# A new stripe order at the end of an input projection, and a denser weave of modulation columns

## The chip, the cores and the metric

The kernel runs on one core of one Trainium2 chip. The metric is the device time of one execution in microseconds; lower is better.

## The reference, cut to what matters

One encoder layer is applied with the same weights to a prompt (512 tokens) and a sample (1024 tokens), both 1024 wide. Everything is float32; the kernel holds activations transposed, channels on the partitions.

```
mod = silu(c) @ w_ada + b_ada        # 6 x 1024 per request: shift, scale, gate for mixer and MLP
h   = rmsnorm(x) * (1 + scale_a) + shift_a
[q | k | v | u] = h @ w_in           # 1280 columns = 10 stripes of 128
q, k = rope(rmsnorm per head)        # 8 query heads, 2 key heads, 64 wide
a   = softmax(q k^T / 8) v           # bidirectional
p   = (centred window mean of u - u) @ w_pool * pool_scale
x   = x + gate_a * rmsnorm([a | p] @ w_out)
x   = x + gate_m * rmsnorm(relu(h2 @ w_ff1)^2 @ w_ff2)
```

## The kernel before, in words

Big products are split: weights and activations are each a high and a low part (`wh`, `wl`; `hh`, `hl`), and `block` (L154) adds three 128x512 matmuls for each 128 rows of the contraction: L159 (wh, high), L160 (wh, low), L161 (wl, high). A 128x512 output of 1024 inner rows is 24 matmuls.

The stage that the change touches lies between 102 and 300 us. Three generators are woven together there by `weave`, which advances a background by its rate each time the foreground yields (after every six matmuls):

- the foreground `in_proj_s` (L567), the sample's input projection: 10 stripes of `w_in` in the order of `S_IN`, two halves of 512 tokens each, 20 blocks of 24 matmuls. Stripes 0 to 3 are queries, 4 the keys, 5 the values, 6 to 9 the pooling channels u. A query stripe is followed by `qk_post` (L386): ScalarE copies the block out of PSUM (L377, `xT`), TensorE transposes it (L383, `nat`, in `ps_m` or, every second time, in one half of `s2`), ScalarE squares (L393), VectorE norms and rotates in seven larger operations (L395 to L410, `y`), TensorE transposes back (L383), ScalarE and VectorE split it (L414, L415, `rh`), and ScalarE's queue writes it to DRAM (L419, `q_d`). A pooling stripe is only copied out and written to DRAM (L584, `u_d`).
- `bg`, at a rate of 1.2: `attention(0)`, the prompt's attention, 16 units of two heads. A head's half of a unit is: scores S (L618, two matmuls into the one tile `s2`), a maximum on VectorE (L628, `amx`), an exponential on ScalarE (L630, `p`), the reciprocal (L632) and the scaling by it on ScalarE or VectorE (L634, L636), four transposes on TensorE (L653, `pT`), a split (L656 `ph` on ScalarE, L657 `pl` on VectorE). A unit then ends with eight matmuls with the values (L666, L667, `x`), a copy (L671, `ao`) and a write to DRAM (L672, `a_d`). All of `s2` is one tile: the next scores, and every transpose that `qk_post` puts in its other half, wait for the exponential that reads it.
- `gv`, at a rate of 0.38: `gemv_cols`, 24 columns of the prompt's modulation (the first five steps are empty). A column is one 512 KB load (L268, `g`) and one 128x1024 multiply-and-sum on VectorE (L236).

Behind the weave stand `drain(bg)`, `drain(gv)`, and the prompt's output projection: `out_prep` (L720) reads `p_d` and `a_d` back (L741, L733), adds two halves on VectorE (L734) and splits (`oh` L743, `ol` L744); `out_proj(0, 0)` (L749) is eight blocks of 24 matmuls on these, with `attention(1)`, the sample's attention, woven in at 0.5. Its first scores need the load `q` (L602) of the sample's queries, into a buffer that the prompt's attention had.

The order on each engine is not the order of the code: a scheduler lays the instructions out when the program is built, each engine then runs its own list in order, and an instruction that waits holds up what stands behind it, on a queue that issues DMAs as well. SP issues the loads, ScalarE's queue the writes.

Of the kernel before, what the change touches and what calls it, by code (L numbers as in the profile page):

```python
# [24 lines left out]
def weave(fg, bgs):  # L25

    credit = [0.0] * len(bgs)
    for _ in fg:
        for i, (bg, rate) in enumerate(bgs):
            credit[i] += rate  # L30
            while credit[i] >= 1.0:
                credit[i] -= 1.0
                next(bg, None)


def drain(g):
    for _ in g:
        pass


def chain(*gs):
    for g in gs:
        yield from g
# [3 lines left out]
def hymba_encoder_layer(ctx, tc, xp, xs, ns_, vec, gqk, rope, edge, ident_in, w_ada_c,  # L47
# [99 lines left out]
    def next_w():  # L147

        while w_seq and len(w_ready) < AHEAD + 1:
            w_ready.append(load_w(*w_seq.pop(0)))  # L150
        return w_ready.pop(0)

    def mm_tile():
        return ps_mm.tile([128, 512], F32, tag="mm", name="mm")  # L154

    def block(ps, wh, wl, acts, ks=range(KB)):
        for i, k in enumerate(ks):
            ah, al = acts[k]
            nc.tensor.matmul(ps, lhsT=wh[:, k, :], rhs=ah, start=(i == 0), stop=False)  # L159
            nc.tensor.matmul(ps, lhsT=wh[:, k, :], rhs=al, start=False, stop=False)  # L160
            nc.tensor.matmul(ps, lhsT=wl[:, k, :], rhs=ah, start=False, stop=(i == len(ks) - 1))  # L161
            if i % 2 or i == len(ks) - 1:
                yield
# [94 lines left out]
    def gemv_cols(c, cb, lo=16, hi=48, pool=None):  # L258
        late = []
        for jb in range(lo, hi):  # L260
            if pool is None:
                r = load_raw(w_ada_c[jb])
                gemv_part(c, jb, r, cb, r)
                if jb % 8 == 7:
                    gemv_done(c, jb - 7)
            else:
                r = pool.tile([128, 1024], F32, tag="g", name="g", bufs=2)
                dma(r, w_ada_c[jb])  # L268
                tc.keep_in_program_order(gemv_part(c, jb, r, cb, r))
                if late:  # L270
                    gemv_done(c, late.pop())
                if jb % 8 == 7:
                    late.append(jb - 7)
            yield
        for j0 in late:
            gemv_done(c, j0)
# [98 lines left out]
    def evac(ps, t=None):  # L375
        t = inp.tile([128, 528], F32, tag="pl", name="xT", bufs=3)[:, :512] if t is None else t
        nc.scalar.activation(out=t, in_=ps, func=AF.Copy)  # L377
        return t
# [47 lines left out]
    def v_post(c, hf, xT):  # L426
        t = natural(xT)
        tv = t.rearrange("p (j h d) -> p j h d", j=4, h=2)
        vh = vst[c][:, hf * 4:hf * 4 + 4, :, 0, :]
        vl = vst[c][:, hf * 4:hf * 4 + 4, :, 1, :]  # L430
        nc.scalar.activation(out=vh, in_=tv, func=AF.Copy)
        nc.vector.tensor_tensor(vl, tv, vh.bitcast(F32), AL.subtract)
        yield
# [128 lines left out]
            posts.append(qk_post(0, 0, xs_[b], b))  # L562
        rest.append(rp)

    S_IN = (4, 5, 9, 0, 8, 1, 7, 2, 6, 3)

    def in_proj_s():  # L567
        pend = []
        ws = {}
        for blk, hf in [(b, f) for f in range(2) for b in S_IN[:3]] + [(b, f) for b in S_IN[3:] for f in range(2)]:  # L570
            if hf == 0:
                ws[blk] = next_w()
            wh, wl = ws[blk]
            ps = mm_tile()
            for _ in block(ps, wh, wl, [h_t[1, hf, k] for k in range(KB)]):
                if pend and next(pend[0], 1) == 1:
                    pend.pop(0)
                yield
            if blk < 5:
                pend.append(qk_post(1, hf, evac(ps), blk))  # L580
            elif blk == 5:
                pend.append(v_post(1, hf, evac(ps)))
            else:
                put(u_d[blk - 6, :, hf * 512:(hf + 1) * 512], evac(ps))  # L584
        while pend:
            if next(pend[0], 1) == 1:
                pend.pop(0)
            yield
# [693 lines left out]
    hs0, hs1 = hs[8:14] + hs[0:2], hs[2:8] + hs[14:16]  # L1282
    w_seq += [(w_in[b],) for b in S_IN]
    w_seq += [(w_out[m],) for m in range(KB)]
# [13 lines left out]
    bg = attention(0, att0)  # L1298
    gv = gemv_cols(0, cb0, 16, 40, inp)
    gv = chain([0] * 5, gv)  # L1300
    bg = chain([0] * 6, bg)
    weave(in_proj_s(), [(bg, 1.2), (gv, 0.38)])
    drain(bg)
    drain(gv)
    att0_close()
# [17 lines left out]
    bg = attention(1, att1)  # L1323
# [10 lines left out]
    def gemv_rest():  # L1334
        make_cb(0, cb[:, 0:1024])
        yield from gemv_cols(0, cb[:, 0:1024], 40)
        make_cb(1, cb[:, 0:1024])
        yield from gemv_cols(1, cb[:, 0:1024])
        for g in range(4):
            yield from u_post(1, g, (cb[:, 0:528], cb[:, 528:1056]))  # L1340
    gv = gemv_rest()
# [160 lines left out]
```

## Time and profile before

| what | us |
|---|---|
| median of 3 runs (lowest, highest) | 1666.7 (1665.64, 1670.02) |
| the profiled execution's own time | 1668.83 |
| its span, from first to last instruction | 1665.7 |
| TensorE busy / VectorE / ScalarE in the span | 1611.2 / 1213.7 / 854.8 |

In the profile a line names an engine, a source line, an operation, and what it writes and reads by the program's names; buffer numbers are left out there (`s2` reads `s`, `hh0_3` reads `hh`). "Idle before" is the time the engine stood still ahead of the instruction, and behind the arrow stands what ended it. PEld is the weight load of TensorE, which runs beside its matmuls. SPq and ACTq are the issuing of DMAs on those two queues. PEclk is the clock that TensorE was granted, 1.00 being full speed. Times within the span count from its start.

### The profile page before, as it was taken

The numbers are of one execution on the slowest core, as the hardware profiler recorded it, in microseconds if no ns is written. First come the engines' busy times: TensorE is split into PE (matmuls) and PEld (weight loads), VectorE is DVE, ScalarE is ACT, GpSimd is POOL, SyncE is SP. The second block draws the span as 40 slices with busy tenths as digits, with TensorE's granted clock in tenths as the row PEclk, the third lists the DMA queues.
The fourth block names the chain that finished last, engine by engine and source line by source line (L and its number), as shares of the span: only waits on it lengthen the run. The fifth ranks groups of instructions, "written<-read, shape, count | busy, mean of one in ns | idle before, by whom it ended". The sixth has DMA issues, their size and how long they took to land. (4 is left out here: it accounts for less than half of the span.)

```text
span 1665.7 us, 21550 instructions
## 1 busy us (share of the span) xinstructions
PE 1611.2 (97%) x7680; PEld 1299.9 (78%) x7680; DVE 1213.7 (73%) x1938; ACT 854.8 (51%) x1450; POOL 10.4 (1%) x27
## 2 busy tenths in 40 slices
PE   7999998999999999999999999899999999999996
PEld 4467886788888878888888888788888788888886
DVE  7898988568667675655667487878875576878757
ACT  2446664556645545546453475744445564444433
POOL 0000000000000000000000000000000000000002
PEclk8999999989999999999999999999999999999998
DMA  7756776443555553332368537566663745444334
GB/s 294 279 156 186 224 221 183 146 153 123 166 174 180 165 179 102 100 108 89 99 206 245 178 127 246 195 224 226 225 216 121 237 160 186 140 141 152 93 110 152
DMA packets 150618, 287.57 MB, mean 173 GB/s; under 512 B 15152, under 2 KB 56432, under 8 KB 150512
## 3 DMA queue, kind: packets, MB, share of 16 engines
q1 hardware_dynamic: 125824, 258.31, 47.9%
q10 hardware_dynamic: 24688, 27.89, 5.4%
q8 instruction: 60, 0.98, 0.2%
q14 instruction: 46, 0.38, 0.1%
HBM read 223.20 MB, written 61.37 MB: 171 GB/s over the span
## 5 line engine op out<-in xcount | busy, mean ns | idle before, releaser
L140 DVE TENSOR_TENSOR wl<-raw,wh 128x1024 fp32r<-128x1024 f32 (+2 forms) x106 | 121.1, 1142 | 70.4 <-ACT wh L139 69.9
L139 ACT ACTIVATE wh<-raw 128x1024 fp32r<-128x1024 f32 (+2 forms) x106 | 105.4, 995 | 120.4 <-PE mm L160 91.7
L630 ACT ACTIVATE p<-s,amx 128x1024 f32<-128x1024 f32 (+1 forms) x96 | 93.3, 972 | 108.6 <-DVE amx L628 106.7
L657 DVE TENSOR_TENSOR pl<-pT,ph 128x512 fp32r<-128x512 f32 x160 | 108.6, 686 | 54.8 <-ACT ph L656 54.3
L875 PE MATMUL pa<-fo,wh 128*128 128x512 f32 x448 | 140.4, 395 | 2.7 <-ACT x L1012 2.7
L628 DVE TENSOR_REDUCE amx<-s 128x1 f32<-128x1024 f32 (+1 forms) x96 | 100.1, 1042 | 43.5 <-PE s L618 43.1
L656 ACT ACTIVATE ph<-pT 128x512 fp32r<-128x512 f32 x160 | 93.4, 594 | 46.1 <-PE pT L653 36.8
L159 PE MATMUL mm<-hA,wh 128*128 128x512 f32 x256 | 106.7, 417 | 0.0
L159 PE MATMUL mm<-fh,wh 128*128 128x512 f32 x256 | 106.5, 417 | 0.0
L875 PE MATMUL mm<-fo,wh 128*128 128x512 f32 x336 | 104.8, 393 | 0.0
L875 PEld LDWEIGHTS pa<-fo,wh 128*128 128x128 f32 x448 | 84.8, 189 | 21.9 <-ACT x L1012 3.1
L161 PE MATMUL mm<-fh,wl 128*128 128x512 f32 x256 | 101.3, 396 | 0.0
L160 PE MATMUL mm<-fl,wh 128*128 128x512 f32 x256 | 101.0, 394 | 0.0
L160 PE MATMUL mm<-hA,wh 128*128 128x512 f32 x256 | 100.9, 395 | 0.0
L161 PE MATMUL mm<-hA,wl 128*128 128x512 f32 x256 | 100.5, 394 | 0.0
L653 PE MATMUL pT<-ident,p 128*128 128x128 f32 x640 | 96.6, 275 | 1.4 <-DVE pl L657 0.9
L618 PE MATMUL s<-kst,q 128*128 128x512 f32 x320 | 93.9, 406 | 4.0 <-ACT p L630 2.0
L653 PEld LDWEIGHTS pT<-ident,p 128*128 128x128 f32 x640 | 79.3, 142 | 22.6 <-issue 2.4
L875 PE MATMUL pa<-fo,wl 128*128 128x512 f32 x224 | 88.1, 393 | 0.0
L881 ACT ACTIVATE fo<-raw 128x512 fp32r<-128x512 f32 x106 | 66.3, 631 | 38.3 <-DMA raw<-f_d 31.5
L882 DVE TENSOR_TENSOR fo<-raw,fo 128x512 fp32r<-128x512 f32 x106 | 71.2, 689 | 15.8 <-ACT fo L881 15.2
L666 PE MATMUL x<-ph,vst 128*128 128x256 f32 x320 | 81.7, 285 | 0.5 <-ACT ph L656 0.5
(291 smaller groups left out, 3922.5 us busy)
## 6 DMA issues: line engine op xcount, KB each, us to landing
raw<-in_w_ff SPq DMA_DIRECT2D x56, 512.0 KB, 3.8
f_d<-x SPq DMA_DIRECT2D x98, 256.0 KB, 2.8
raw<-f_d SPq DMA_DIRECT2D x98, 256.0 KB, 3.0
raw<-in_w_ada_c SPq DMA_DIRECT2D x40, 512.0 KB, 3.9
g<-in_w_ada_c SPq DMA_DIRECT2D x24, 512.0 KB, 4.3
q<-q_d SPq DMA_DIRECT2D x96, 128.0 KB, 3.6
raw<-in_w_out SPq DMA_DIRECT2D x24, 512.0 KB, 3.8
rawx<-in_w_ff SPq DMA_DIRECT2D x20, 512.0 KB, 4.0
```

The source lines that it names most:

```text
L139: nc.scalar.activation(out=fh, in_=r[:, :n], func=AF.Copy)
L140: nc.vector.tensor_tensor(fl, r[:, :n], fh.bitcast(F32), AL.subtract)
L159: nc.tensor.matmul(ps, lhsT=wh[:, k, :], rhs=ah, start=(i == 0), stop=False)
L160: nc.tensor.matmul(ps, lhsT=wh[:, k, :], rhs=al, start=False, stop=False)
L161: nc.tensor.matmul(ps, lhsT=wl[:, k, :], rhs=ah, start=False, stop=(i == len(ks) - 1))
L618: nc.tensor.matmul(s[:, f * 512:(f + 1) * 512], lhsT=q[:, h, p, :], rhs=kst[c][:, kv, f * 512:(f + 1) * 512].bitcast(F32R), start=(p == 0) ...
L628: nc.vector.tensor_reduce(mx, s[:, :n], AX.X, AL.max, negate=True)
L630: nc.scalar.activation(out=pr, in_=s[:, :n], func=AF.Exp, bias=mx, accum_out=den)
L653: nc.tensor.transpose(t[:, k, :], pr[:, (4 * f + k) * 128:(4 * f + k + 1) * 128], ident)
L656: nc.scalar.activation(out=hi, in_=t, func=AF.Copy)
L657: nc.vector.tensor_tensor(lo, t, hi.bitcast(F32), AL.subtract)
L875: nc.tensor.matmul(ps, lhsT=x[:, k, :], rhs=y, start=start and k == i == 0, stop=k == n - 1 and i == 2, skip_group_check=not start)
```

## The change

Stripe order in the last four places goes from 7, 2, 6, 3 to 2, 7, 3, 6, so that the last block is pooling stripe 6 and the last query stripe, 3, comes one stripe earlier; and the modulation columns are woven in at 0.5 instead of 0.38. No instruction is added or taken away.

```diff
-    S_IN = (4, 5, 9, 0, 8, 1, 7, 2, 6, 3)
+    S_IN = (4, 5, 9, 0, 8, 1, 2, 7, 3, 6)
...
     gv = chain([0] * 5, gv)
     bg = chain([0] * 6, bg)
-    weave(in_proj_s(), [(bg, 1.2), (gv, 0.38)])
+    weave(in_proj_s(), [(bg, 1.2), (gv, 0.5)])
     drain(bg)
     drain(gv)
```

Since a scheduler sets the order, the two edits move rows on all engines of this stage. From the place that the profile before has at 322 us on, and ahead of 102 us, the lists are the same.

First place: TensorE at the end of the input projection. `mm_2743` is the last block before and `mm_2808` now, `mm_2987` and `mm_3044` are blocks 0 and 1 of `out_proj(0, 0)`, and `nat` rows are transposes of a query stripe. Before:

```order
L160 MATMUL mm_2743<-hl1_7_1003,wh_2306 128x512
L161 MATMUL mm_2743<-hh1_7_1002,wl_2307 128x512
L383 MATMUL nat_2810<-ident_96,xT_2808 128x128 x4
L159 MATMUL mm_2987<-oh_2925,wh_2502 128x512
L159 MATMUL mm_3044<-oh_2925,wh_2697 128x512
L383 MATMUL nat_2798<-ident_96,y_2783 128x128 x4
L160 MATMUL mm_2987<-ol_2926,wh_2502 128x512
```

And now: the first rows from the projection's last matmul on, and five from a little further down. Units 13, 14 and 15 of `attention(0)`, the last three, have the value products `x_2601`, `x_2699` and `x_2749`:

```order
L161 MATMUL mm_2808<-hh1_7_1002,wl_2345 128x512
L618 MATMUL s2_172<-kst0_169,q_2426 128x512 x2
L666 MATMUL x_2601<-ph_2429,vst0_167 128x256
L653 MATMUL pT_2588<-ident_96,p_2546 128x128 x4
L667 MATMUL x_2601<-pl_2430,vst0_167 128x256
```

```order
L618 MATMUL s2_172<-kst0_169,q_2536 128x512 x2
L653 MATMUL pT_2643<-ident_96,p_2584 128x128 x4
L666 MATMUL x_2699<-ph_2539,vst0_167 128x256
L667 MATMUL x_2699<-pl_2540,vst0_167 128x256
L383 MATMUL s2_172<-ident_96,xT_2630 128x128 x4
```

What moved: before, all of `attention(0)` stood ahead of the projection's last matmuls; now three of its 32 scores, four of its 32 groups of transposes and the last three units' value matmuls stand behind them, without a matmul of a projection between, and `out_proj(0, 0)` begins only behind the last of these and a last `nat`. Both orders have three `nat` rows behind the projection's last matmul.

Second place: TensorE at the first scores of `attention(1)`, `s_2999`. Before, it stood in the third block of `out_proj(0, 0)` (`mm_3093`), behind 63 matmuls of that projection:

```order
L159 MATMUL mm_3093<-oh_2949,wh_2983 128x512
L160 MATMUL mm_3093<-ol_2950,wh_2983 128x512
L161 MATMUL mm_3093<-oh_2949,wl_2984 128x512
L618 MATMUL s_2999<-kst1_168,q_2919 128x512 x4
L159 MATMUL mm_3093<-oh_2958,wh_2983 128x512
```

Now it stands in the first block, behind 12:

```order
L159 MATMUL mm_2987<-oh_2940,wh_2555 128x512
L160 MATMUL mm_2987<-ol_2941,wh_2555 128x512
L161 MATMUL mm_2987<-oh_2940,wl_2556 128x512
L618 MATMUL s_2999<-kst1_168,q_2919 128x512 x4
L159 MATMUL mm_2987<-oh_2949,wh_2555 128x512
```

Third place: SP's queue, which issues the loads. `q_2536` is the query tile of the last unit of `attention(0)`, `q_2919` that of the first unit of `attention(1)`, `raw_2923` reads back what the last four units wrote, `g` rows are modulation columns. Before:

```order
L733 DMA accA3_2912<-a_d0_83 64x512 x2
L268 DMA g_2754<-in_w_ada_c 128x1024
L733 DMA raw_2923<-a_d0_83 64x512 x4
L128 DMA raw_2981<-in_w_out 128x1024
L128 DMA raw_3038<-in_w_out 128x1024
L602 DMA q_2919<-q_d1_82 64x4x128 x2
```

And now:

```order
L602 DMA q_2536<-q_d0_81 64x4x128 x2
L733 DMA accA3_2912<-a_d0_83 64x512 x2
L733 DMA raw_2922<-a_d0_83 64x512 x3
L733 DMA raw_2923<-a_d0_83 64x512 x4
L602 DMA q_2919<-q_d1_82 64x4x128 x2
L602 DMA q_2994<-q_d1_82 64x4x128 x2
L128 DMA raw_2981<-in_w_out 128x1024
```

What moved: the last columns are loaded earlier, the last loads of `attention(0)` stand among those of `out_prep`, and the queries of `attention(1)` stand ahead of the two weight loads, right behind `raw_2923`.

## The prediction

> **What bounds the kernel now.** I read the page first, then the stage's windows, then TensorE's timeline, then SP's and ScalarE's queues.
>
> ```profile
> PE 1611.2 (97%) x7680; PEld 1299.9 (78%) x7680; DVE 1213.7 (73%) x1938; ACT 854.8 (51%) x1450; POOL 10.4 (1%) x27
> ...
> core 0: us, PE busy (x) PEld busy (x) DVE busy (x) ACT busy (x) POOL busy (x), PEclk, DMA share, GB/s
> 102.00:274.00 172.00, 169.72 (x904) 138.24 (x902) 151.00 (x320) 103.23 (x216) 0.00 (x0) 1.00 0.70 211
> ...
> 274.30:282.60 8.30, 1.96 (x11) 1.45 (x11) 6.99 (x21) 5.51 (x13) 0.00 (x0) 0.83 0.44 132
> 282.60:286.60 4.00, 4.00 (x11) 3.16 (x10) 4.00 (x9) 0.60 (x1) 0.00 (x0) 0.50 0.23 47
> 286.60:299.20 12.60, 12.60 (x57) 9.92 (x55) 5.79 (x9) 2.82 (x5) 0.00 (x0) 1.00 0.73 202
> 299.20:301.00 1.80, 0.03 (x1) 0.01 (x1) 0.86 (x1) 1.80 (x3) 0.00 (x0) 1.00 0.68 223
> ```
>
> TensorE is the bound: 97% of the span, 169.72 of 172 us in the input projection. Its work is the same after the change, so only its waits and its clock can move. The one hole nearby is at the hand-over to the output projection: 1.96 us of work in 8.30, then 4.00 us at clock 0.50. Who makes it:
>
> ```profile
> start us, us, engine line op out<-in xcount [idle before <-releaser]
> 273.91 0.40 PE L161 MATMUL mm<-hh,wl 128*128 128x512 f32 x1
> 275.86 0.66 PE L383 MATMUL nat<-ident,xT 128*128 128x128 f32 x4 [1.55 <-ACT xT L377]
> ...
> 281.90 1.08 PE L383 MATMUL nat<-ident,y 128*128 128x128 f32 x4 [4.79 <-DVE rs_t L173]
> ...
> 292.94 0.40 PE L159 MATMUL mm<-oh,wh 128*128 128x512 f32 x1
> ...
> 298.85 0.39 PE L161 MATMUL mm<-oh,wl 128*128 128x512 f32 x1
> 301.02 1.16 PE L618 MATMUL s<-kst,q 128*128 128x512 f32 x4 [1.79 <-DMA q<-q_d]
> ```
>
> The projection ends at 273.91 + 0.40 = 274.3. TensorE then waits 1.55 us for the last query block's copy and 4.79 us for its norm and rotation; at 301.0 it waits 1.79 us for the first queries of `attention(1)`. Together 8.1 us, and 2.0 us of the 4.00 at half clock: at most 10.1 us to be won. Matmuls run 26 steps in 298.85 - 292.94, 0.227 us each.
>
> **The change part by part.**
>
> *The last stripe.* A pooling block leaves a copy and a write, no work for VectorE or TensorE. But the last `nat` of query stripe 3 now stands behind the remainder of `attention(0)`, so the query block's tail isn't gone, it is behind another. I give it no gain.
>
> *What falls behind the projection.* Three scores, four groups of transposes, three units' 24 value matmuls. Their pitch:
>
> ```profile
> 254.91 0.60 PE L653 MATMUL pT<-ident,p 128*128 128x128 f32 x4
> 255.26 0.48 PE L618 MATMUL s<-kst,q 128*128 128x512 f32 x1
> ...
> 256.42 0.39 PE L618 MATMUL s<-kst,q 128*128 128x512 f32 x1
> ...
> 259.63 0.63 PE L618 MATMUL s<-kst,q 128*128 128x512 f32 x2
> 260.10 0.39 PE L161 MATMUL mm<-hh,wl 128*128 128x512 f32 x1
> ...
> 265.01 0.28 PE L667 MATMUL x<-pl,vst 128*128 128x256 f32 x1
> ...
> 270.44 0.28 PE L666 MATMUL x<-ph,vst 128*128 128x256 f32 x1
> 270.56 0.28 PE L667 MATMUL x<-pl,vst 128*128 128x256 f32 x1
> ```
>
> 0.47 for a scores pair, 0.35 for four transposes, 0.12 for a value matmul: 3 x 0.47 + 4 x 0.35 + 24 x 0.12 = 5.7 us. So the projection ends at 274.3 - 5.7 = 268.6, if TensorE is as full as before until there. After that it has these 5.7 us and three `nat` to do, one chain without cover. Its length, step by step, until the first scores of `attention(1)`:
>
> 1. VectorE's list has the addition of `raw_2922` (L734) ahead of a reciprocal that the next exponentials are queued behind. Its three loads stand on SP behind two loads of `q_2536`, which wait until the second scores of unit 13 free their buffer, 5.9 us ahead of the projection's end (15 projection matmuls at 0.227, 8 value matmuls, two groups of transposes, one `nat`, a scores pair): 262.7. Seven issues follow (two of `q`, two of `accA`, three of `raw`), and a landing:
>
> ```profile
> 267.84 4.28 SPq L733 DMA_DIRECT2D accA<-a_d  x4
> ...
> 275.18 2.36 SPq L733 DMA_DIRECT2D raw<-a_d  x4
> ...
> 289.35 3.22 SPq L128 DMA_DIRECT2D raw<-in_w_out  x2
> 292.62 3.76 SPq L602 DMA_DIRECT2D q<-q_d  x4
> ...
> raw<-a_d SPq DMA_DIRECT2D x8, 128.0 KB, 3.1
> q<-q_d SPq DMA_DIRECT2D x8, 128.0 KB, 7.3
> accA<-a_d SPq DMA_DIRECT2D x8, 128.0 KB, 4.9
> ...
> DMA to landing us min/median/max: 2.7/6.7/7.7
> ...
> L734 DVE TENSOR_TENSOR raw<-raw 128x512 f32<-128x512 f32 x1 | 0.7, 692 | 0.0
> ```
>
> (The last column of the DMA rows is the median from issue to landing; the row of minimum, median and maximum is that of the `q` loads.) An issue is 2.36 / 4 = 0.59 to 4.28 / 4 = 1.07 us. At 0.8 an issue, 3.1 to land and 0.7 to add, the addition ends at 262.7 + 5.6 + 3.1 + 0.7 = 272.1, 3.5 us behind the projection's end (2.0 with the short issue, 7.2 with the long one and 4.9 to land).
>
> 2. From there to the last scores: two more scores and one group of transposes take turns in `s2`, each behind the exponential of the one before. Scores followed each other like this:
>
> ```profile
> 248.85 0.70 PE L618 MATMUL s<-kst,q 128*128 128x512 f32 x2
> 251.22 0.66 PE L618 MATMUL s<-kst,q 128*128 128x512 f32 x2
> ...
> 271.32 0.66 PE L383 MATMUL s<-ident,xT 128*128 128x128 f32 x4 [0.48 <-ACT xT L377]
> ...
> L393 ACT ACTIVATE sqh<-s 128x512 f32<-128x512 f32 x6 | 3.6, 596 | 1.6 <-DMA g<-in_w_ada_c 1.2 <-PE s L383 0.3
> ```
>
> That is 2.4 us, then 4.0 and 4.4 to 255.26 and 259.63. Two links are 4.8 to 8.8 us, and the transposes with their square 0.66 + 0.60 = 1.3 between them; I take 6.5, near the short end, because no columns stand in VectorE's list any more, and keep 6.1 to 10.1.
>
> 3. From the last scores to the unit's last value matmul: 260.3 to 270.8 for unit 15 before, 10.6 us (8.5 for unit 14: 256.8 to 265.3). I take 10.6, since the rotations of two query blocks now stand beside it in VectorE's list; 8.5 at the low end, and at the high end 13.4, with one rotation's four operations of 0.69 in its way:
>
> ```profile
> L409 DVE TENSOR_TENSOR y<-y,tabs 128x512 f32<-128x512 f32 x11 | 7.5, 685 | 0.1
> L236 DVE CUSTOM_DVE_ANT_0 g<-g,cb 128x1024 f32<-128x1024 f32 x23 | 28.0, 1216 | 2.3 <-DMA g<-in_w_ada_c 2.3
> ```
>
> (The second row is a modulation column; it is used below.)
>
> 4. The last unit's way through DRAM. ScalarE's copy and write, then SP:
>
> ```profile
> 271.17 0.38 ACT L671 ACTIVATE ao<-x 128x256 f32<-128x256 f32 x1
> 272.36 0.38 ACTq L672 DMA_DIRECT2D a_d<-ao  x1
> ```
>
> From 270.8 to the end of the four `raw` issues at 275.18 + 2.36 = 277.5, 6.7 us. The queries of `attention(1)` stand right behind on SP.
>
> 5. Two issues of these, 1.5 us, and the landing. The median in this stretch is 7.3 us, but with two 512 KB weight loads ahead of them, which now stand behind; I take the 3.1 us of the 128 KB reads `raw<-a_d`: 4.6. The ends are 1.2 + 2.7 = 3.9 and 1.9 + 7.7 = 9.6. One rule bears on this step. The Trainium skill, "DMA: Bandwidth & Descriptors", section "Anatomy of one DMA", puts a transfer at about 2.0 us fixed plus bytes over 436 GB/s, fitted on loads that GpSimd issues. By that a 128 KB read would take an estimated 2.3 us and the sum below would be 0.8 us lower; the trace doesn't agree here, 3.1 us in the median, and I go by the trace.
>
> Sum: 3.5 + 6.5 + 10.6 + 6.7 + 4.6 = 31.9 us, so the scores `s_2999` run at 268.6 + 31.9 = 300.5, as early as before (301.0). But 63 matmuls of `out_proj(0, 0)` stood ahead of them before and 12 do now: 51 x 0.227 = 11.6 us of TensorE work is still to come that was done. Behind `s_2999` both orders are dense with matmuls, as 286.60:299.20 is. TensorE enters it after some 5 us of waiting, and 4.79 us before cost 2.0 us at half clock (0 to 2.0). In all 300.5 - 301.0 + 11.6 + 2.0 = +13.1 us. All low ends make a chain of 2.0 + 6.1 + 8.5 + 6.7 + 3.9 = 27.2, and without a cold clock 295.8 - 301.0 + 11.6 = +6.4; all high ones make 47.0 and +28.2.
>
> *Columns at 0.5.* 24 columns at 1.2 us are VectorE work in either order; they come up to four columns earlier, and push six head-halves of attention back. TensorE was covered before (169.72 of 172 us), with VectorE at 151.00. I cost it at nothing ahead of the projection's end, covered by the projection's own matmuls, which stand in the list between.
>
> *SP's queue.* The first weight loads of `out_proj`'s third block come later. They wait for the same tiles and TensorE reaches them later by the same time; nothing.
>
> The sum stands against the profiled execution (span 1665.7, 1668.83 in all); applied to the median of 1666.7 it gives 1679.8, and I say 1679.
>
> **The rivals.** A measurement here tells about 0.3%, 5 us, from no change.
>
> *Slower, as worked out:* 1679; its own range is 1673, with all low ends, to 1688, a little over half-way to all high ones, which will hardly fall together.
>
> *Faster: the hand-over closes.* The holes of 8.1 us and the half clock of 2.0 us go and nothing takes their place: 1657. For it: stripe 3's rotation really has a stripe more of cover in its first half. It decides at `s_2999`: for no loss it has to run at 301.0 - 11.6 = 289.4, 20.8 us behind the projection's end, and for 5 us of gain at 284.4, 15.8 us. The low ends of the chain make 27.2.
>
> *No measurable change.* The chain runs near its low ends (`raw_2922` is there in time, rotations fall into gaps): 1673 by the low ends, and 1670 if two steps overlap by 3 us. VectorE was only busy 6.99 of 8.30 us in the old hole, which speaks for some of it.
>
> *Slower still: VectorE becomes the bound within the projection.* Four columns earlier are 4 x 1.3 = 5.2 us more VectorE work ahead of the attention's, and the projection's end moves by as much: 1684. Against it: the order keeps projection matmuls between.
>
> **How the numbers follow.** Slower as worked out 0.66; slower with stalls within the projection 0.12; no measurable change 0.14; faster 0.08. So faster 0.08, same 0.14, slower 0.78. The range 1667 to 1688 leaves out the faster case (0.08), a part of the unchanged one (0.04) and the highest sums (0.08).
>
> **What would show it.** Right: TensorE's projection ends near 268.6 and behind it come some 30 us with less than 13 us of work, waiting for `p`, `y`, `pl` and for the load of `q`; the granted clock near 0.5 at its end; `s_2999` near 300; the first value matmul of `attention(1)` some 13 us later than its place in the profile before; from there on the same intervals. Each step has its row: the addition of `raw_2922` near 272, the last scores of `attention(0)` near 278.5, its last value matmul near 289, SP's queries near 297. It would be wrong if the last value matmul came before 280, or if `s_2999` didn't wait.

## The result, and the profile after

The changed kernel takes 1678.67 us in the median of four runs (1676.17 to 1680.58), the kernel before 1667.62 us in its four (1665.64 to 1670.02): a ratio of 1.0059, 95% interval 1.0040 to 1.0079. It is slower by 11 us in the medians (9.8 by the ratio, 6.7 to 13.2), where 13 were forecast. The profiled execution, the quickest of the four, took 1676.17 us (span 1674.2), against 1668.83 (1665.7).

TensorE's busy time on the page of the changed kernel:

```profile
PE 1615.4 (96%) x7680; PEld 1303.9 (78%) x7680; DVE 1213.4 (72%) x1938; ACT 854.5 (51%) x1450; POOL 10.4 (1%) x27
```

The work is the same, instruction for instruction, and takes 4.2 us more (1611.2 before), at a mean granted clock of 0.981 for 0.984. The rest of the longer span is waiting. TensorE's timeline of the changed kernel, from the last matmul of the input projection to the first scores of `attention(1)`:

```profile
266.74 0.39 PE L161 MATMUL mm<-hh,wl 128*128 128x512 f32 x1
268.31 0.73 PE L618 MATMUL s<-kst,q 128*128 128x512 f32 x2 [1.18 <-ACT p L630]
...
271.04 0.91 PE L653 MATMUL pT<-ident,p 128*128 128x128 f32 x4 [1.86 <-ACT p L634]
...
273.24 1.05 PE L618 MATMUL s<-kst,q 128*128 128x512 f32 x2
...
277.92 0.72 PE L618 MATMUL s<-kst,q 128*128 128x512 f32 x2
...
284.23 1.09 PE L383 MATMUL nat<-ident,y 128*128 128x128 f32 x4 [5.35 <-DVE y L410]
285.11 1.06 PE L653 MATMUL pT<-ident,p 128*128 128x128 f32 x4
...
289.03 0.41 PE L667 MATMUL x<-pl,vst 128*128 128x256 f32 x1
...
293.96 0.79 PE L159 MATMUL mm<-oh,wh 128*128 128x512 f32 x1 [3.67 <-ACT oh L743]
...
298.90 0.40 PE L161 MATMUL mm<-oh,wl 128*128 128x512 f32 x1
299.70 1.17 PE L618 MATMUL s<-kst,q 128*128 128x512 f32 x4 [0.40 <-DMA q<-q_d]
```

The reader sees the chain of the prediction: three scores at 268.3, 273.2 and 277.9, taking turns in `s2` with the exponentials that read it; then a `nat` that waits 5.35 us for a query block's rotation, with the last unit's transposes queued behind it; the last value matmul at 289.0; 3.67 us for the first operand of `out_proj(0, 0)`; and the scores at 299.7, a little earlier than the 301.02 of before, but with only 12 matmuls of `out_proj(0, 0)` done ahead of them instead of 63. The waits between 266.7 and 299.7 sum to 14.2 us, against 8.1 in the same hand-over before.

What that costs is seen at the next common place, the first value matmul of `attention(1)`, before and then after:

```profile
322.23 0.28 PE L666 MATMUL x<-ph,vst 128*128 128x256 f32 x1
```

```profile
332.37 0.28 PE L666 MATMUL x<-ph,vst 128*128 128x256 f32 x1
```

That is 10.1 us. ScalarE's square at L214, near 875 us, is 9.7 us later, and the profiled span 8.5 us longer, so a little over a microsecond is given back in between in that execution. Ahead of the hand-over nothing was lost: the projection's end is 1.5 us earlier than worked out.

One number sums up a hand-over below: the start of the first scores of `attention(1)`, less 0.227 us for each matmul of `out_proj(0, 0)` that the order has ahead of them. It is the time at which those scores would have run with nothing of that projection done, half clock included. Before it is 301.0 - 63 x 0.227 = 286.7; after it is 299.7 - 12 x 0.227 = 297.0, 10.3 later. I call it the mark.

### The profile page after: what moved, and what is told of

The parts are those of the page before. It is cut to its first block, busy times and chain, and to the rows that moved or that the text cites. A ratio compares the mean times of both kernels' runs of the same rounds, so it can differ in the third digit from the quotient of the medians.

```text
span 1674.2 us, 21552 instructions
## 1 busy us (share of the span) xinstructions
PE 1615.4 (96%) x7680; PEld 1303.9 (78%) x7680; DVE 1213.4 (72%) x1938; ACT 854.5 (51%) x1450; POOL 10.4 (1%) x27
## 5 line engine op out<-in xcount | busy, mean ns | idle before, releaser
L667 PE MATMUL x<-pl,vst 128*128 128x256 f32 x320 | 82.8, 290 | 1.2 <-DVE pl L657 1.0
```

## Experiments

All twelve ran in five rounds beside the kernel before, in three groups of four (before: 1669.79, 1669.91 and 1669.45 us). Marks and places are those of each kernel's one profiled execution; "last scores" and "last value matmul" are those of `attention(0)`.

| kernel | ratio (95%) | projection ends | last scores | last value matmul | mark against before |
|---|---|---|---|---|---|
| before | 1 | 274.3 | 259.6 | 270.6 | 0 |
| the change | 1.0059 (1.0040 to 1.0079) | 267.1 | 277.9 | 289.0 | +10.3 |
| e1 stripes alone | 1.0020 (1.0003 to 1.0037) | 273.6 | 268.3 | 282.7 | +5.2 |
| e2 columns alone | 1.0017 (1.0002 to 1.0031) | 270.3 | 270.5 | 278.6 | +2.7 |
| e3 attention at 2 | 1.0049 (1.0032 to 1.0066) | 279.4 | 244.5 | 250.9 | +7.2 |
| e4 columns at 0.25 | 1.0046 (1.0030 to 1.0061) | 275.5 | 262.9 | 274.8 | +5.4 |
| e5 attention six steps earlier | 0.9995 (0.9976 to 1.0014) | 276.4 | 268.6 | 277.4 | -0.1 |
| e6 transposes out of `s2` | 1.0016 (1.0001 to 1.0031) | 279.0 | 271.6 | 281.9 | +2.1 |
| e7 16 columns later, new stripes | 1.0008 (0.9992 to 1.0023) | 274.9 | 269.6 | 280.2 | +4.4 |
| e8 16 columns later, old stripes | 1.0012 (0.9997 to 1.0027) | 272.1 | 256.4 | 265.0 | -5.8 |
| e9 attention six steps later | 1.0006 (0.9988 to 1.0023) | 268.0 | 270.5 | 280.2 | +0.2 |
| e10 new stripes, four earlier | 1.0004 (0.9986 to 1.0021) | 277.9 | 263.0 | 275.4 | +0.3 |
| e11 old stripes, four earlier | 1.0009 (0.9994 to 1.0024) | 274.7 | 258.5 | 272.3 | +2.6 |
| e12 8 columns later, four earlier | 1.0017 (0.9997 to 1.0036) | 284.9 | 260.9 | 273.9 | +4.3 |

### The two edits apart

The new stripe order with the old rate (e1):

```diff
-    weave(in_proj_s(), [(bg, 1.2), (gv, 0.5)])
+    weave(in_proj_s(), [(bg, 1.2), (gv, 0.38)])
```

> Only the new stripe order; columns stay at 0.38. In this build's lists no scores of attention(0) stand behind the projection's last matmul, one group of transposes and 8 value matmuls do, and the first scores of attention(1) stand behind 12 matmuls of out_proj(0,0), as in the changed kernel. Uncovered tail (the price is the length of the attention(0) chain behind the projection, less the out_proj matmuls that can stand in it): the last scores lie some 4.5 us ahead of the projection's end at 273.0, so the last value matmul comes near 279 to 280, the first scores of attention(1) near 290, and 51 matmuls are still to come: +0 us, 1667.6 (-3 to +4). Columns alone cost: the same as before, 1667.6. Stripe order alone costs: the whole +11, 1678.6.

And the old order with the new rate (e2):

```diff
-    S_IN = (4, 5, 9, 0, 8, 1, 2, 7, 3, 6)
+    S_IN = (4, 5, 9, 0, 8, 1, 7, 2, 6, 3)
```

> Only the columns at 0.5; the old stripe order. In this build one scores pair, three groups of transposes and 16 value matmuls of attention(0) stand behind the projection's last matmul, and the first scores of attention(1) behind 65 matmuls of out_proj(0,0), as before. Uncovered tail: the projection ends at 270.9, the last value matmul comes about 11 us later, near 282, and out_proj(0,0) begins near 284 to 285 instead of 282.6, with nothing owed behind it: +1 to +4 us, 1670. Columns alone cost: the whole +11, 1678.6. Stripe order alone costs: 1667.6.

Each costs about 3 us (3.3 and 2.8 by the ratios, with intervals of 0.5 to 6.2 and 0.3 to 5.2). By the mark they cost 5.2 and 2.7, together 7.9 of the 10.3. So neither edit is the culprit alone; each pushes the last scores of `attention(0)` back, from 259.6 to 268.3 and 270.5, and both together to 277.9. The columns, which the prediction costed at nothing ahead of the projection's end, cost through that. TensorE's timeline of e1 also shows what the new stripe order does by itself:

```profile
268.83 0.66 PE L653 MATMUL pT<-ident,p 128*128 128x128 f32 x4
...
277.87 1.09 PE L383 MATMUL nat<-ident,y 128*128 128x128 f32 x4 [4.29 <-DVE rs_t L174]
278.75 1.06 PE L653 MATMUL pT<-ident,p 128*128 128x128 f32 x4
...
289.35 0.79 PE L159 MATMUL mm<-oh,wh 128*128 128x512 f32 x1 [3.69 <-ACT oh L743]
```

The old wait for a query block's norm and rotation (4.79 us before) is still there (4.29), only for the stripe that now comes earlier, and the last unit's transposes are queued behind it. The prediction gave the new last stripe no gain for this reason.

### Attention ahead of the projection's end

If attention behind the projection is the loss, pulling it ahead must remove it. First by rates, both edits kept: attention at 2.0 (e3), or columns at 0.25 (e4).

```diff
-    weave(in_proj_s(), [(bg, 1.2), (gv, 0.5)])
+    weave(in_proj_s(), [(bg, 2.0), (gv, 0.5)])
```

> Both edits of the change kept, and attention(0) woven in at 2.0 instead of 1.2. In this build all of attention(0) stands ahead of the last 100 matmuls of the projection; behind them only three transposes of a query block remain, and 60 matmuls of out_proj(0,0) stand ahead of the first scores of attention(1). Uncovered tail: the loss is gone, and with the query block's tail a stripe earlier a part of the old hole of 8 us too: -7 to +1 us, 1660 to 1669. Columns alone or stripe order alone cost: both are still there, so the loss stays, 1676 to 1681.

```diff
-    weave(in_proj_s(), [(bg, 1.2), (gv, 0.5)])
+    weave(in_proj_s(), [(bg, 1.2), (gv, 0.25)])
```

> The new stripe order with the columns at 0.25. In this build nothing of attention(0) and one transpose group stand behind the projection's last matmul, and 99 matmuls of out_proj(0,0) stand ahead of the first scores of attention(1). About 8 of 24 columns come behind the projection. Uncovered tail: no loss, and the old hole of 8 us mostly closed: -8 to -2 us, 1660 to 1666, unless the late columns hold the buffers of attention(1) and make a new wait there. Columns cost: a little below before, 1665 to 1668. Stripe order alone costs: 1678.6.

Both expectations failed: 8.2 and 7.7 us slower than before, although attention is done 28 us (e3) and 0.5 us (e4) ahead of the projection's end. TensorE's timeline and the window from 250 to 300 us of e3:

```profile
281.21 0.63 PE L383 MATMUL nat<-ident,y 128*128 128x128 f32 x4 [1.86 <-DVE rs_t L174]
288.23 1.09 PE L383 MATMUL nat<-ident,y 128*128 128x128 f32 x4 [6.39 <-DVE qrs L175]
288.97 0.78 PE L159 MATMUL mm<-oh,wh 128*128 128x512 f32 x1
```

```profile
250.00:300.00 50.00, 39.36 (x180) 31.21 (x181) 43.79 (x99) 18.66 (x41) 0.00 (x0) 0.90 0.73 221
```

and the same window of the changed kernel (columns: window, length, then busy us of PE, PEld, DVE, ACT and POOL, PEclk, DMA share, GB/s):

```profile
250.00:300.00 50.00, 35.69 (x164) 28.27 (x163) 36.07 (x79) 23.73 (x52) 0.00 (x0) 0.80 0.51 150
```

VectorE has 43.79 us of work there in e3, against 36.07: its list there holds eight columns for one and the operations of six rotations for four, and these and the additions of `out_prep` are now the queue at the hand-over. VectorE's list of e4 shows columns in it, waiting for their loads, with the operand of `out_proj` behind them:

```profile
284.95 1.22 DVE L236 CUSTOM_DVE_ANT_0 g<-g,cb 128x1024 f32<-128x1024 f32 x1 [3.81 <-DMA g<-in_w_ada_c]
286.10 0.08 DVE L236 DVE_READ_ACCUMULATOR2_ANT mod<- 128x1 f32 x1
286.21 0.17 DVE L249 TENSOR_TENSOR mod<-mod,vt 128x8 f32<-128x8 f32 x1
286.30 1.28 DVE L744 TENSOR_TENSOR ol<-accA,oh 128x512 fp32r<-128x512 f32 x2
```

TensorE's row that waits for that `ol`:

```profile
287.04 0.80 PE L160 MATMUL mm<-ol,wh 128*128 128x512 f32 x1 [5.12 <-DVE ol L744]
```

So the two kernels have other holes at the same place; these causes are read from the traces and were not tried apart. They say that "attention done in time" is not enough for no loss.

Next by place alone: both edits and both rates kept, the empty steps ahead of attention left out (e5).

```diff
-    bg = chain([0] * 6, bg)
+    bg = chain([0] * 0, bg)
```

> Both edits kept; the prompt's attention begins six steps earlier (its six empty steps are left out). The last scores of attention(0) then stand 20 projection matmuls ahead of the projection's end, only the last unit's 8 value matmuls behind it, and 63 matmuls of out_proj(0, 0) ahead of the first scores of attention(1), as before the change. If the loss is the uncovered chain of scores and exponentials behind the projection, most of it goes: 0 to +4 us against the kernel before, first value matmul of attention(1) at 322 to 326. If it is VectorE's backlog at the hand-over (the rotations of the query stripe that comes earlier, and columns), which the place of attention(0) does not change, it stays at +6 to +10, as with attention(0) at a rate of 2.

The whole loss is gone: 0.9995 (0.9976 to 1.0014), mark -0.1, and the first value matmul of `attention(1)` at 322.07, as before (322.23). This is the cleanest answer of the study: with both edits in place, moving attention forward by six steps of its weave removes the loss, to within some 3 us either way. TensorE's timeline of e5 at the hand-over:

```profile
268.57 0.62 PE L618 MATMUL s<-kst,q 128*128 128x512 f32 x2
...
277.40 0.28 PE L667 MATMUL x<-pl,vst 128*128 128x256 f32 x1
...
279.84 1.22 PE L159 MATMUL mm<-oh,wh 128*128 128x512 f32 x2 [2.16 <-ACT oh L743]
282.40 0.80 PE L160 MATMUL mm<-ol,wh 128*128 128x512 f32 x1 [1.34 <-DVE ol L744]
```

The last scores run 9.4 us earlier than in the changed kernel, the last value matmul 11.6, the first matmul of `out_proj` 14.1; and projection matmuls stand between the last scores and the last value products.

Then by the turns in `s2` (e6): a query stripe's transposes always go to their own bank.

```diff
-        t = natural(xT, ps_m, "m") if n_post[0] % 2 else natural(xT, out=s2[:, 512:1024])
+        t = natural(xT, ps_m, "m")
```

> Both edits kept; all transposes of a query stripe go to their own bank, none into the half of s2 that takes turns with the scores. In the order all of attention(0) but the last 8 value matmuls then stands ahead of the projection's end. If the turns in s2 are what pushed three units behind the projection, the loss goes down to 0 to +5 us against before. If the one bank for the transposes of two halves is the tighter thing, transposes wait for the squares and norms of the block before, and the loss stays at +6 to +12 with waits of nat inside the projection.

1.0016 (1.0001 to 1.0031): 2.7 us slower than before, so some three quarters of the loss are gone, and the last scores run at 271.6 for 277.9. The turns that scores and transposes take in one tile are part of what pushed attention back, if the new layout that comes with the edit did nothing else; that was not parted.

### A tail without the edits

The kernel before, with attention six steps later (e9):

```diff
-    bg = chain([0] * 6, bg)
+    bg = chain([0] * 12, bg)
-    weave(in_proj_s(), [(bg, 1.2), (gv, 0.5)])
+    weave(in_proj_s(), [(bg, 1.2), (gv, 0.38)])
```

(and the old `S_IN`; the diff is against the changed kernel.)

> Neither edit: stripe order and column rate as before, but the prompt's attention begins six steps later (12 empty steps for 6). Two of its scores, four groups of transposes and 16 value matmuls now stand behind the projection (4.3 us of work), and 65 matmuls of out_proj(0, 0) ahead of the first scores of attention(1). If the uncovered chain is enough by itself: projection's end near 270, last scores some 5 us later, last value matmul 10.6 us behind them, near 286, out_proj from 286 to 290 for 282.6 before: +4 to +9 us. If it takes the new stripe order or the columns: -1 to +2.

This missed: 1.0006 (0.9988 to 1.0023), no loss that can be measured. TensorE's timeline of e9:

```profile
267.60 0.39 PE L161 MATMUL mm<-hh,wl 128*128 128x512 f32 x1
...
270.49 0.73 PE L618 MATMUL s<-kst,q 128*128 128x512 f32 x2 [0.23 <-ACT p L630]
...
280.16 0.42 PE L667 MATMUL x<-pl,vst 128*128 128x256 f32 x1
282.12 1.22 PE L159 MATMUL mm<-oh,wh 128*128 128x512 f32 x2 [1.55 <-ACT oh L743]
284.21 1.09 PE L383 MATMUL nat<-ident,y 128*128 128x128 f32 x4 [0.87 <-DVE y L410]
285.06 0.79 PE L160 MATMUL mm<-ol,wh 128*128 128x512 f32 x1
```

The projection ends within a microsecond of where the change has it, and 4.3 us of attention stand behind it, two scores for three. But the last scores start 2.5 us behind the projection's end, not 10.8: the two followed each other in 2.3 us (268.18 and 270.49). From there to the last value matmul it is 9.7 us, for 11.1 in the changed kernel, and the query block's `nat` stands behind the value matmuls, not ahead of the last transposes. So attention behind the projection is not a loss by itself. In e9 its tail ends within the old hole: `out_proj` begins at 282.1, and before its matmuls were dense only from 282.6 on. Nor does the time of the last scores alone tell the loss (268.3 in e1 with a mark of +5.2, 270.5 in e9 with +0.2): what stands between them and `out_proj`, which began at 289.4 in e1 and at 294.0 in the changed kernel, counts as much. The size of the tail in matmuls, by which the expectation was made, tells little.

### Fewer columns, and a version that beats both

16 of the 24 columns moved into `out_proj(0, 0)`, with the new (e7) and the old (e8) stripe order and rate:

```diff
-    gv = gemv_cols(0, cb0, 16, 40, inp)
+    gv = gemv_cols(0, cb0, 16, 24, inp)
...
-    weave(out_proj(0, 0), [(bg, 0.5)])
+    cbx = f0p.tile([128, 1024], F32, name="cbx")
+    make_cb(0, cbx)
+    gv = gemv_cols(0, cbx, 24, 40, f0p)
+    weave(out_proj(0, 0), [(bg, 0.5), (gv, 0.6)])
+    drain(gv)
```

> Both edits kept, but only 8 of the 24 modulation columns are in this stage; 16 are woven into out_proj(0, 0) at 0.6, with eight more small matmuls to spread the vector again. 19 us of VectorE work and 16 loads of 512 KB leave the stage. If the loss is the uncovered chain: one group of transposes and 8 value matmuls still stand behind the projection and 13 matmuls of out_proj ahead of the first scores of attention(1), so +1 to +6 against before. If it is VectorE's backlog: -3 to +2. If VectorE has no room in out_proj(0, 0) either, its operands ol, the weights' low parts and the maxima come late there: over +6.

> The kernel before with 16 of its 24 columns moved into out_proj(0, 0) at 0.6, stripe order and rates as before. The hand-over of before waits 1.5 us for a copy and 4.8 us for a norm and rotation on VectorE. If VectorE's load makes that hole, it shrinks: -3 to -8 us against before. If the norm's own chain (transpose, square, sum, norm, rotation, transpose) makes it, 0 to -2. With no room for the columns in out_proj(0, 0): +2 to +8.

e8 shows a hand-over nearly closed: its two `nat` wait 0.69 and 1.58 us where they waited 1.55 and 4.79, and the mark is 5.8 us earlier than before, as its first theory had it for the time, so the columns (their work on VectorE or their loads; the two weren't parted) made much of the old hole. But the kernel isn't faster (1.0012, 0.9997 to 1.0027, 2.0 us slower in the middle, the edge of its third theory): the gain is given back, most visibly in the next 150 us. The windows of before, then of e8:

```profile
300.00:350.00 50.00, 47.91 (x254) 39.99 (x254) 29.01 (x37) 29.96 (x52) 0.00 (x0) 1.00 0.40 130
350.00:400.00 50.00, 48.57 (x279) 43.05 (x280) 41.39 (x64) 32.43 (x60) 0.00 (x0) 0.86 0.34 110
400.00:450.00 50.00, 48.44 (x266) 40.75 (x265) 34.62 (x50) 29.47 (x50) 0.00 (x0) 1.00 0.57 176
```

```profile
300.00:350.00 50.00, 46.92 (x252) 39.43 (x250) 44.24 (x68) 26.56 (x47) 0.00 (x0) 0.97 0.81 262
350.00:400.00 50.00, 46.51 (x253) 41.04 (x252) 38.75 (x59) 28.83 (x53) 0.00 (x0) 0.80 0.33 107
400.00:450.00 50.00, 47.25 (x250) 39.60 (x249) 31.81 (x45) 28.70 (x50) 0.00 (x0) 0.97 0.51 157
```

TensorE is busy 140.7 us of the 150 there, against 144.9; VectorE has 44.24 us of work in the first 50 where it had 29.01. The rest of the way back was not traced. e7 keeps both edits and ends at 1.0008 (0.9992 to 1.0023), with the mark still 4.4 late; two of its theories allow that time, so it doesn't choose between them. The last three were tries at a better version: attention four steps earlier with columns at 0.38, in the new order (e10) and the old (e11), and the new order with 8 columns moved (e12, at 0.25, columns in the stage at 0.5).

```diff
-    bg = chain([0] * 6, bg)
+    bg = chain([0] * 2, bg)
```

> New stripe order, columns at 0.38, the prompt's attention four steps earlier (2 empty steps for 6). All of attention(0) stands ahead of the projection's end, its last value matmul nine projection matmuls ahead of it, no transposes of a query block ahead of out_proj(0, 0), 65 matmuls of it ahead of the first scores of attention(1). If the chain was all of the loss, the new stripe order may now show its gain: the old holes of 6.3 us at the hand-over go down to the operands of out_proj, -2 to -6 us against before. If those operands (oh, ol behind attention's trip through DRAM) take the place of the wait: -1 to +2.

> Old stripe order, columns at 0.38, the prompt's attention four steps earlier. The last query block's transposes, norm and rotation stay behind the projection's end. If that block's own tail makes the hole of before: 0 to -2 us against before. If attention's remainder on VectorE made part of it: -3 to -6.

> New stripe order, columns at 0.5 but only 16 of them in this stage, 8 woven into out_proj(0, 0) at 0.25, the prompt's attention four steps earlier. All of attention(0) is done 39 projection matmuls ahead of the projection's end, no transposes stand behind it, and 21 matmuls of out_proj(0, 0) ahead of the first scores of attention(1). If the place of attention(0) and VectorE's load are the whole of the hand-over: -3 to -7 us against before. If columns beside attention(1) cost what 16 of them seem to have (about 2 to 5 us given back): -2 to +2.

None is faster than before. e10 has the hand-over that was looked for (no `nat` ahead of `out_proj`) and its mark is +0.3: the operands took the wait's place (2.4 us for `ol`, 1.2 for `oh`), as its second theory said. e11 waits 4.8 us for a `nat` behind VectorE, as before. e12 lost 5.0 us to a single wait for `pl` within the projection, which ends at 284.9; on VectorE that `pl` stands behind an addition (L734) that waits 3.49 us for its load of `raw`, the same thing that the prediction named in its step 1. e11 and e12 came out 1.5 and 2.8 us slower in the middle, above the ranges of all their theories. No version that beats the kernel before was found; e5 is the changed kernel without its loss.

Over the eleven kernels whose columns stay in the stage (before and the change among them), the mark gives the measured difference (the ratio less 1, times the time of before) within 2.3 us. With columns moved it doesn't: it was 3.0 and 1.4 us above the measured difference for e7 and e12, and 7.8 below for e8.

## Why the prediction was right

It was right in direction and size and nearly in every place. That 1679 was forecast and 1678.67 measured is in part luck: the sum was 2 to 3 us too high, and the kernel before came out at 1667.62 for the 1666.7 that it was added to. Within the sum, the early end of the projection and the long step 2 are off against each other:

| step | forecast | measured |
|---|---|---|
| the projection ends | 268.6 | 267.1 |
| 1. addition of `raw_2922` ends, behind that | +3.5 | +3.0 (270.2) |
| 2. to the last scores' end | +6.5 | +8.5 (278.6) |
| 3. to the unit's last value matmul | +10.6 | +10.8 (289.4) |
| 4. to SP's queries | +6.7 | +6.2 (295.7) |
| 5. to `s_2999` | +4.6 | +4.0 (299.7) |
| sum of the five steps | 31.9 | 32.6 (267.1 to 299.7, steps rounded) |
| matmuls owed behind `s_2999` | +11.6 | 63 - 12 = 51, +11.6 |
| half clock behind it | +2.0 | 0 |
| in all | +13.1 | +10.3 by the mark, +10.1 in the trace, +11.05 in the medians |

*Step 1* stands in VectorE's list of the changed kernel, and its cause in SP's:

```profile
267.43 0.69 DVE L734 TENSOR_TENSOR accA<-accA,accA 128x512 f32<-128x512 f32 x1 [2.17 <-DMA raw<-a_d]
269.47 0.69 DVE L734 TENSOR_TENSOR raw<-raw 128x512 f32<-128x512 f32 x1 [1.35 <-DMA raw<-a_d]
270.07 0.16 DVE L632 RECIPROCAL aden<-aden 128x1 f32<-128x1 f32 x1
```

```profile
260.97 1.19 SPq L602 DMA_DIRECT2D q<-q_d  x2
262.20 1.29 SPq L733 DMA_DIRECT2D accA<-a_d  x2
263.54 32.03 SPq L733 DMA_DIRECT2D raw<-a_d  x7
295.67 2.50 SPq L602 DMA_DIRECT2D q<-q_d  x4
```

The loads do stand behind `q_2536`, the addition does wait for its load, and the reciprocal runs right behind it. In e9, where no addition that waits for a load stands there, the second-last score follows without a stop. The row of 32.03 us holds the three loads of `raw_2922`, a long wait, and the four of `raw_2923`; the queries follow at 295.67.

*Step 2* was taken 2.0 us too short, within its ends. It was taken near the short one because no columns stand in VectorE's list any more; the scores came at pitches of 4.9 and 4.7 us (268.31, 273.24, 277.92), longer than any of the rows shown. With the columns gone, the turn through maximum, exponential, reciprocal, scaling and transposes was left, and it took as long. About 1 us of it is half clock, by an estimate from TensorE's rows: from 271.04 to the second scores at 273.24, four transposes and seven value matmuls took 2.20 us, where the prediction's pitches make 0.35 + 7 x 0.12 = 1.2.

*Step 3* came out at its size, by a way that was named only in part: the two rotations do lie in between, but what shows on TensorE is one `nat` that waits 5.35 us for the first of them and holds the last unit's transposes. Their operand was ready at 282.0 (scaled from 281.48, 0.48 long), the transposes ran at 285.1: that order may have cost up to 3.1 us, which no run tried apart.

*The half clock* is the term that was mis-sized: 2.0 us forecast, none measured behind `s_2999`. It was put behind the scores, and it lies ahead of them. The windows of the changed kernel:

```profile
275.00:285.00 10.00, 3.63 (x23) 3.16 (x23) 7.92 (x24) 5.18 (x14) 0.00 (x0) 0.83 0.07 21
285.00:300.00 15.00, 10.10 (x31) 7.28 (x30) 9.11 (x16) 6.55 (x12) 0.00 (x0) 0.55 0.59 157
300.00:305.00 5.00, 5.00 (x23) 4.11 (x22) 2.11 (x3) 2.83 (x5) 0.00 (x0) 1.00 0.53 189
```

The 12 matmuls of `out_proj(0, 0)` from 293.96 on ran at about half clock (mostly 0.43 us apart for 0.227) and ended at 299.3, when the queries were landing anyway; the wait left for them was 0.40 us. So these slow matmuls were paid out of a wait, and the clock was 1.00 again when the debt began. One sign that the prediction named did not come: "less than 13 us of work" behind the projection. TensorE was busy for 18.3 of the 32.6 us, at a granted clock of 0.69; the work had been counted at full clock.

*Columns at 0.5: nothing* holds for the stretch ahead of the projection's end, of which it was said, but not for the edit as a whole (e2: +2.8 us, interval 0.3 to 5.2). The sum did not miss it, since their effect is the place of attention, which the sum took from the order. The rival "slower still by VectorE within the projection" did not happen: no stall within it moved its end. The rival "the hand-over closes" needed the scores at 289.4 and they came at 299.7.

What stays open is which VectorE work, and in which order, would close the hand-over without a wait elsewhere: e3, e4, e11 and e12 were 1.5 to 8 us slower than before in the middle of their intervals, by waits for one operand or another (`y`, `ol`, `pl`), and each of these was read from one trace.

## What to carry to other kernels

Where one product ends and the next begins, look for the last chain of small dependent steps and ask which matmuls stand beside it: work that was hidden costs its latency once nothing stands beside it, not its busy time, so count the turns (scores, exponential, reciprocal, transposes) and not the matmuls, and set against it the hole that was there already (e9). A change of order is priced at the first place where both orders have done the same work: take the time there, less what each has already done of the next product. When a rate is changed in a weave, every stream's end moves; the same two edits lost 11 us or nothing depending on six empty steps at the start of another stream.

## What the runs showed of the hardware

TensorE's clock fell without a long pause. In e9 no wait of TensorE in this stretch was longer than 1.84 us, and these are its windows:

```profile
274.00:277.00 3.00, 1.13 (x8) 0.84 (x8) 2.57 (x6) 1.67 (x5) 0.00 (x0) 1.00 0.19 61
277.00:282.00 5.00, 2.60 (x10) 1.86 (x8) 5.00 (x19) 2.54 (x9) 0.00 (x0) 0.55 0.01 5
282.00:288.00 6.00, 5.01 (x15) 3.50 (x16) 5.64 (x11) 3.78 (x8) 0.00 (x0) 0.52 0.37 109
```

A stretch of several short waits with 1.13 us of work in 3.00 was followed by a clock of 0.55 and 0.52 for some ten microseconds. The Trainium skill, "TensorE: Matmul & The Clock Gate", in the section "Why this matters for your kernels", says to allow no idle gap of more than about 3 us between bursts of matmuls; by that rule alone e9 would have kept its clock. The trace differs. The changed kernel shows it too: its longest wait between 267.1 and 271.0 is 1.86 us, and from 271.0 to 273.5 the clock was 0.56.

What decides is open. How little was done over a few microseconds fits e9 and the changed kernel, but not every trace. In e11 a wait of 1.58 us ended at 298.15 with matmuls close together on both sides of it, and the clock was 0.51 from 299.9 to 303.2. In the kernel before, the wait of 1.79 us that ended at 301.02 was followed by a clock of 1.00 (301 to 309). So waits of about the same length did both, and no run was made for it.
